# Gated-projection blocks placed inside the last batches of the state-space head, with the weight tiles in the input stage's space and W4 on another queue

## Chip, cores, metric
One core of a Trainium2 chip. The metric is device time in microseconds for one launch, median over runs; the kernel is one program with no loop at run time, every instruction is laid out in order per engine.

## What is computed
Two transformer blocks on 256 tokens of width 2048, all in float32. Only the first half of the first block is touched here: a state-space mixer (S5) followed by a gated projection.

```
sh1, sc1, gt1, sh2, sc2, gt2 = split(silu(c) @ w_mod + b_mod, 6)
h   = rms_norm(x) * (1 + sc1) + sh1                      # also for the context tokens
for both directions:  s_t = lam * s_(t-1) + B u_t        # 128 groups of 16 channels, 64 complex states
                      y  += real(C s_t)
z   = gelu(y + d * u)
a, g = split(z @ w_glu, 2)                               # w_glu is 2048 x 4096
x   = x + gt1 * rms_norm(a * sigmoid(g))
h   = rms_norm(x) * (1 + sc2) + sh2                      # goes into a 2048-8192-2048 MLP, then gt2
```

## The kernel before
**The head** (`head`, L139). The 128 groups are done in four batches of 32. A batch `b` has four generators from `s5_batch` (L375): `m` modulates the input (needs the modulation vectors from `mod_matmul`), `e` builds the input matrices X, transposes them and multiplies them with u in eight steps, `s` is the scan over chunks on DVE, `z` makes the outputs in eight steps. ORDER (L41) says in what order the program calls them; "e2+z0" alternates a step of each. The head stands in a block whose instructions a planner then reorders: it simulates the timeline and gives each engine its next ready instruction, earlier program order first.

One step of `z` (L556 to L592): DVE builds Z (three products, L403); ACT copies parts of B into bm (L566); PE multiplies bm with Z into a bank `pk` (L571, L575); ACT copies that to Kp (L578); four DMAs of 64 KB each spread Kp into the tile W4 (L582, on ACT's queue); ACT copies the states into SN (L585, L586). Two steps later (ZLAG = 2) `product` (L544) multiplies Z, SN, u and W4 into a bank `py` (L552) and ACT applies the gelu (L554). `pk`, `py` and the final transposes share the two banks of the tag "py". When a batch is through, PE transposes its result (L598) and ACT and DVE split it into a high part `zh` (L604) and a low part `zl` (L605). These are four of the sixteen k-tiles that the gated projection multiplies with; they are listed in `za`.

Beside this the head computes the vectors gt1 and sc2 (`mod_vectors`, L291): 32 steps, each with two loads of 512 KB and eight matmuls (L303), called from `z` by the digits of WORK (L36): two per step of batches 0 and 1.

**The dense part** (`Dense`, L611). Weights stream in chunks of 512 KB (`load`, L618): SP issues the load into a `raw` tile (L681), ACT casts it to the high half `wh` (L628), DVE subtracts for the low half `wl` (L629), PE does three matmuls for each pair of tiles (L657): a chunk is 24 matmuls of 128x256. `block` (L647) does one 512-wide block of outputs in eight chunks. The gated projection (L893 to L903) is three pairs of 512-wide blocks and two pairs of 256-wide ones: 64 chunks, 1536 matmuls. `glu_out` (L861) evicts a pair. `dn.fill` (L850) puts a step of `ModVectors.steps` (L330) after every second chunk: a 512 KB load `wv` on SP, and a multiply-and-sum on DVE (L338) for the vector sh2, 32 steps. The vector `cond` that it needs is loaded and put through Silu at L327 and L328, after the head.

**Memory.** In the head `raw` has four tiles that all weight loads share; after it another pool `raw2` has six. PSUM: four banks "ps" (used by `m` and `e`), two "py", two "ab" (`mod_matmul`, `mod_vectors`); after the head a new pool takes all eight.

Of the kernel before, what the change touches and what calls it, by code (L numbers as in the profile page):

```python
# [35 lines left out]
WORK = ("22222222", "22222222", "00000000", "00000000")  # L36
# [3 lines left out]
DPOOL = "BCEG"  # L40
ORDER = "m0:1 e0:4 c0 m0 e0 m1:1 s0 e1:4 m1 e1 m2 e2+z0:4 s1 m3 e2+z0 e3+z1:4 s2 e3+z1 s3 z2 z3"  # L41


class K:
    def __init__(self, ctx, tc, aps):
# [4 lines left out]
        self.psp = None  # L50
# [88 lines left out]
def head(k, raw, ctx):  # L139
# [17 lines left out]
    with ExitStack() as bx:  # L157
        b1, b2 = (bx.enter_context(tc.tile_pool(name=f"b{n}", bufs=n, reuse_waits="tile")) for n in (1, 2))
        pools = b1, b2, b3
# [21 lines left out]
        for b in range(NB):  # L181
            for i in range(2):
# [137 lines left out]
class ModVectors:  # L320


    def __init__(self, k, pool):
        self.k, nc, c = k, k.nc, k.a["c"]
        self.part = {v: k.cp.tile([P, 2, KT], F32, name=f"mvp{v}") for v in (3, 5)}
        self.cond = pool.tile([P, 2, 1024], F32, tag="hid", name="cond")
# [3 lines left out]
    def steps(self, raw, v):  # L330

        nc = self.k.nc
        for kt in range(KT):
            for h in range(2):
                t = raw.tile([P, 1024], F32, tag="raw", name=f"wv{v}_{kt}_{h}")
# [39 lines left out]
def s5_batch(k, pools, act, za, b, rs, ub, Q, R, WP, dd, bms, acc, ahead, work):  # L375

    nc, a = k.nc, k.a
    b1, b2, b3 = pools
# [5 lines left out]
    def build(tag, s, pw, pd, m, conj):  # L384
# [6 lines left out]
        else:  # L391
            out = [b3.tile([P, 4, L * 16], F32, tag=tag, name=f"{tag}{b}_{s}_{t}", bufs=XBUFS) for t in range(3)]
# [14 lines left out]
    def modulate():  # L407
        Bt = tl["B"] = b2.tile([P, 3, GB, 16], F32, tag="B", name=f"B{b}", bufs=3)
        Bx = tl["Bx"] = b2.tile([P, GB, 16], F32, tag="Bx", name=f"Bx{b}")
        nc.scalar.dma_start(Bt[:, 0:2], a["s5_b"][b])  # L410
        qd = tl["qd"] = b2.tile([P, GB, L], F32, tag="qd", name=f"qd{b}")
# [44 lines left out]
    def inputs():  # L456
        EC = tl["EC"] = b1.tile([P, NC_, 2, GB], F32, tag="EC", name=f"EC{b}")
        EL = tl["EL"] = b2.tile([P, NC_, 2, GB], F32, tag="EL", name=f"EL{b}", bufs=3)
        for s in range(GB // 4):
            X = build("X", s, Q, tl["qd"], (tl["Bx"], tl["B"][:, 2], tl["B"][:, 1]), False)  # L460
            W1 = []
            for t in range(3):
# [3 lines left out]
                w = b3.tile([P, 4, P], F32, tag="W1", name=f"W1{b}_{s}_{t}", bufs=4)  # L466
# [60 lines left out]
    def outputs():  # L527
# [28 lines left out]
        for s in range(GB // 4):  # L556
# [23 lines left out]
            for q in range(4):  # L580
                v = Kp[32 * q : 32 * q + 16, 7:15, :]
                nc.scalar.dma_start(W4[:, q, :], bass.AP(v.tensor, v.offset, [v.ap[0], [-16, L], [1, P]]))  # L582
# [10 lines left out]
        for w in wait:  # L593
            product(*w)
        pzs = [k.ps("py") for _ in range(2)]
# [15 lines left out]
class Dense:  # L611
# [20 lines left out]
    def preload(self, src, n=3, wide=512):  # L632

        self.ahead = [self.load(src, i * (1024 // wide), wide) for i in range(n)]
# [12 lines left out]
    def block(self, src, acts, pre=None, wide=512):  # L647

        k, nc = self.k, self.k.nc
        acc = [k.ps() for _ in range(wide // T)]  # L650
        nk = len(acts)
        for kt, hi, lo in self.chunks(src, nk, wide, pre):
            xh, xl = acts[kt]
            for nt in range(wide // P):
                o = acc[nt // 2][:, (nt % 2) * T : (nt % 2 + 1) * T]
                for i, (w, x) in enumerate(((hi, xh), (hi, xl), (lo, xh))):
                    nc.tensor.matmul(o, lhsT=w[:, nt * P : (nt + 1) * P], rhs=x,  # L657
                                     start=(kt == 0 and nt % 2 == 0 and i == 0),
                                     stop=(kt == nk - 1 and nt % 2 == 1 and i == 2))
        return acc  # L660

    def block_t(self, src, acts):
# [11 lines left out]
        return acc  # L674

# [87 lines left out]
def body(ctx, tc, aps):  # L763
# [5 lines left out]
    k.psum(hx, "psh", {"ps": 4, "py": 2, "ab": 2})  # L769
# [8 lines left out]

    with hx:
        k.ctx_head = hx  # L780
        raw = hx.enter_context(tc.tile_pool(name="raw", bufs=4))
        with tc.block(schedule_with_timeline_sim=True):
            za, vecs, act = head(k, raw, ctx)
# [640 lines left out]
```

## Time and profile before

| | us |
|---|---|
| median of three runs | 3377.5 |
| lowest, highest | 3375.14, 3381.65 |
| the profiled execution | 3383.99 |
| its span | 3382.1 |
| mean granted TensorE clock of the span | 0.981 |

A clock of 1.00 is 2.4 GHz, one of 0.50 is 1.2 GHz, a value between them is a mixture over the stretch. Engines: PE is the matmul, PEld the load of its stationary operand, DVE, ACT and POOL the elementwise engines, SP issues DMAs; a "q" behind the name is the engine's queue of instructions that don't compute. "[3.33 <-DMA W<-Kp]" behind a row says how long the engine was idle before it and what ended that. The program's names lose trailing digits: W is W4 and W1, wv the loads of modulation weights, wm those of `mod_matmul`.

### The profile page before, as it was taken

The numbers are of one execution on the slowest core, as the hardware profiler recorded it, in microseconds if no ns is written. First come the engines' busy times: TensorE is split into PE (matmuls) and PEld (weight loads), VectorE is DVE, ScalarE is ACT, GpSimd is POOL, SyncE is SP. The second block draws the span as 40 slices with busy tenths as digits, with TensorE's granted clock in tenths as the row PEclk, the third lists the DMA queues.
The fourth block names the chain that finished last, engine by engine and source line by source line (L and its number), as shares of the span: only waits on it lengthen the run. The fifth ranks groups of instructions, "written<-read, shape, count | busy, mean of one in ns | idle before, by whom it ended". The sixth has DMA issues, their size and how long they took to land.

```text
span 3382.1 us, 69851 instructions
## 1 busy us (share of the span) xinstructions
PE 3217.1 (95%) x30126; PEld 3080.4 (91%) x30126; DVE 2049.5 (61%) x2699; ACT 1461.2 (43%) x1785; POOL 213.0 (6%) x117
## 2 busy tenths in 40 slices
PE   7989669899999999989999999999999999999998
PEld 3567559889999999988999999999999999999998
DVE  8688736785565555689555545555556455555555
ACT  4345445444444434435544434434444443443343
POOL 0000010110000000167300000000000000000000
PEclk9999779999999999989999999999999999999999
DMA  9855267756767565445455555555535555565553
GB/s 311 286 177 177 44 196 272 242 164 230 237 229 231 187 187 187 161 152 166 158 172 187 186 188 186 188 187 187 187 120 187 176 187 187 187 187 187 187 186 139
DMA packets 355141, 642.01 MB, mean 190 GB/s; under 512 B 23184, under 2 KB 94608, under 8 KB 354448
## 3 DMA queue, kind: packets, MB, share of 16 engines
q1 hardware_dynamic: 331824, 620.19, 55.7%
q10 hardware_dynamic: 23008, 17.37, 2.3%
q8 instruction: 235, 3.85, 0.4%
q14 instruction: 74, 0.61, 0.0%
HBM read 626.96 MB, written 2.10 MB: 186 GB/s over the span
## 4 chain that ended last, share of the span: by engine, by line
PE 54%; DVE 1%; issue 0%; ACT 0%; POOL 0%; DVEq 0%; ACTq 0%; POOLq 0%
PE ps L657 52%; PE ps L672 1%; PE ps L1269 0%; POOL wl L629 0%; PE ps L746 0%; DVE xT L1243 0%; PE ps L759 0%; PE ps L1294 0%; PE ps L1053 0%; PE ps L1130 0%; DVE pq L1286 0%; PE ps L1048 0%; PE ps L66 0%; DVE fl L1307 0%; DVE wl L629 0%
## 5 line engine op out<-in xcount | busy, mean ns | idle before, releaser
L629 DVE TENSOR_TENSOR wl<-wr,wh 128x1024 fp32r<-128x1024 f32 x907 | 1115.6, 1232 | 1022.8 <-ACT wh L628 1022.1
L628 ACT CAST wh<-wr 128x1024 fp32r<-128x1024 f32 x976 | 1023.0, 1049 | 1503.6 <-PE ps L657 1372.9
L657 PE MATMUL ps<-f,wh 128*128 128x256 f32 x5632 | 997.2, 280 | 0.0
L657 PEld LDWEIGHTS ps<-f,wh 128*128 128x128 f32 x5632 | 862.3, 188 | 0.1
L657 PE MATMUL ps<-f,wl 128*128 128x256 f32 x2816 | 789.9, 281 | 0.0
L657 PEld LDWEIGHTS ps<-f,wl 128*128 128x128 f32 x2816 | 529.2, 188 | 0.0
L657 PE MATMUL ps<-m,wh 128*128 128x256 f32 x2048 | 366.4, 281 | 8.8 <-DVE m L939 5.7
L657 PE MATMUL ps<-hd,wh 128*128 128x256 f32 x2048 | 360.6, 280 | 0.0
L657 PEld LDWEIGHTS ps<-m,wh 128*128 128x128 f32 x2048 | 315.2, 189 | 10.9 <-DVE m L939 7.0
L657 PEld LDWEIGHTS ps<-hd,wh 128*128 128x128 f32 x2048 | 312.7, 188 | 0.0
L657 PE MATMUL ps<-m,wl 128*128 128x256 f32 x1024 | 287.7, 281 | 0.0
L657 PE MATMUL ps<-hd,wl 128*128 128x256 f32 x1024 | 286.7, 280 | 0.0
L657 PE MATMUL ps<-f1d,wh 128*128 128x256 f32 x1408 | 249.0, 280 | 0.0
L657 PE MATMUL ps<-f0d,wh 128*128 128x256 f32 x1408 | 247.9, 280 | 0.0
L657 PEld LDWEIGHTS ps<-f1d,wh 128*128 128x128 f32 x1408 | 215.3, 188 | 0.0
L657 PEld LDWEIGHTS ps<-f0d,wh 128*128 128x128 f32 x1408 | 215.0, 188 | 0.0
L657 PE MATMUL ps<-f1d,wl 128*128 128x256 f32 x704 | 197.3, 280 | 0.0
L657 PE MATMUL ps<-f0d,wl 128*128 128x256 f32 x704 | 197.1, 280 | 0.0
L657 PEld LDWEIGHTS ps<-m,wl 128*128 128x128 f32 x1024 | 193.2, 189 | 0.0
L657 PEld LDWEIGHTS ps<-hd,wl 128*128 128x128 f32 x1024 | 192.6, 188 | 0.0
L657 PE MATMUL ps<-z,wh 128*128 128x256 f32 x1024 | 184.4, 283 | 7.6 <-ACT wh L628 7.6
L629 POOL TENSOR_TENSOR wl<-wr,wh 128x1024 fp32r<-128x1024 f32 x69 | 167.7, 2441 | 113.6 <-ACT wh L628 106.5
(479 smaller groups left out, 4434.4 us busy)
## 6 DMA issues: line engine op xcount, KB each, us to landing
wr<-in_ffn_w_gate_dram SPq DMA_DIRECT2D x176, 512.0 KB, 3.5
wr<-in_ffn_w_up_dram SPq DMA_DIRECT2D x176, 512.0 KB, 3.5
wr<-in_ffn_w_down_dram SPq DMA_DIRECT2D x176, 512.0 KB, 3.6
wr<-in_w_mlp_in_dram SPq DMA_DIRECT2D x128, 512.0 KB, 4.2
wr<-in_w_mlp_out_dram SPq DMA_DIRECT2D x128, 512.0 KB, 4.5
wv<-in_w_mod_dram SPq DMA_DIRECT2D x64, 512.0 KB, 5.3
wr<-in_s_w_glu_dram SPq DMA_DIRECT2D x64, 512.0 KB, 5.2
wv<-in_w_modt_dram SPq DMA_DIRECT2D x64, 512.0 KB, 4.6
```

The source lines that it names most:

```text
L628: nc.scalar.copy(hi, t)
L629: self.low(n).tensor_tensor(lo, t, hi.bitcast(F32), op=ALU.subtract)
L657: nc.tensor.matmul(o, lhsT=w[:, nt * P : (nt + 1) * P], rhs=x, start=(kt == 0 and nt % 2 == 0 and i == 0), stop=(kt == nk - 1 and nt % 2 = ...
L672: nc.tensor.matmul(acc[tt], lhsT=x[:, tk], rhs=w, start=(kt == 0 and i == 0), stop=(kt == nk - 1 and i == 2))
```

## The change
The gated projection's first three blocks are started inside the head. After `e3+z1` the item "w" closes a pool `xw` (into which X, W1, Bx and qd have moved) and opens the pool `wp` of weight halves in its space. From then on a side step "g" is called once per round: it loads one chunk and does its 24 matmuls for k-tiles that are already in `za`, for the first or second block (banks "ps"), or, when both vectors are done, for the third (banks "ab"). In the last batch two side steps "v" per round do `ModVectors` for sh2, whose `cond` is now loaded at the start of the head. By the order of calls 20 chunks and 22 steps of sh2 fall into the head. W4 of batches 2 and 3 is issued by SP. The scan s3 alternates with z2. WORK spreads the steps of `mod_vectors` over batches 0, 1 and 2 (8, 16, 8). After the head, blocks preload two chunks of the next block before the eviction of a pair; the sums of squares of x go from POOL to DVE (DPOOL) and are moved.

```diff
-WORK = ("22222222", "22222222", "00000000", "00000000")
+WORK = ("11111111", "22222222", "11111111", "00000000")
-DPOOL = "BCEG"
-ORDER = "m0:1 e0:4 c0 m0 e0 m1:1 s0 e1:4 m1 e1 m2 e2+z0:4 s1 m3 e2+z0 e3+z1:4 s2 e3+z1 s3 z2 z3"
+DPOOL = "BEG"
+SIDE = {"g": 1, "v": 2}
+ORDER = "m0:1 e0:4 c0 m0 e0 m1:1 s0 e1:4 m1 e1 m2 e2+z0:4 s1 m3 e2+z0 e3+z1:4 s2 e3+z1 w s3+z2+g z3+g+v"
...
+        if self.ring:
+            tag = self.ring[0]
+            self.ring = self.ring[1:] + self.ring[:1]
...
+        xx = ctx.enter_context(ExitStack())
+        xw = xx.enter_context(tc.tile_pool(name="xw", bufs=1, side="right", reuse_waits="tile"))
+        pools = b1, b2, b3, xw
...
+        vec = k.vec = ModVectors(k)
...
+        side = {}
         for item in ORDER.split():
+            if item == "w":
+                xx.close()
+                side["g"] = start(za, lambda: len(vecs) == 2)
+                side["v"] = k.vec_work = vec.steps(3)
+                continue
             names, n = (item.split(":") + ["99"])[:2]
-            gens = [bt[int(t[1])][t[0]] for t in names.split("+")]
+            names = names.split("+")
+            gens = [bt[int(t[1])][t[0]] for t in names if t not in side]
             for _ in range(int(n)):
                 gens = [g for g in gens if not next(g, 1)]
+                for t in names:
+                    for _ in range(SIDE[t] if t in side else 0):
+                        next(side[t], None)
+                if not gens:
+                    break
...
-                nc.scalar.dma_start(W4[:, q, :], ...)
+                (nc.sync if b >= 2 else nc.scalar).dma_start(W4[:, q, :], ...)
...
         for w in wait:
             product(*w)
+        yield
...
-    def preload(self, src, n=3, wide=512):
+    def preload(self, src, n=3, wide=512, first=0):
...
+class Run:
+    def __init__(self, dn, src, nk, wide=512, tag="ps"):
+        self.dn, self.src, self.nk, self.wide, self.kc = dn, src, nk, wide, 0
+        self.acc = [dn.k.ps(tag) for _ in range(wide // T)]
+    def step(self, acts, pre=None):
+        dn, nc = self.dn, self.dn.k.nc
+        st = 1024 // self.wide
+        hi, lo = dn.ahead.pop(0) if dn.ahead else dn.load(self.src, self.kc, self.wide)
+        if pre:
+            pre(self.kc)
+        if dn.fill:
+            dn.fill()
...
+        self.kc += st
...
-    k.psum(hx, "psh", {"ps": 4, "py": 2, "ab": 2})
+    k.psum(ctx, "psh", {"ps": 4, "py": 2, "ab": 2})
...
+    def start(za, free):
+        dn = Dense(k, raw, ctx.enter_context(tc.tile_pool(name="wp", bufs=3, side="right", reuse_waits="tile")))
+        dense.append(dn)
+        while True:
+            if len(runs) < 2:
+                runs.append(Run(dn, glu_srcs[len(runs)], KT))
+            run = next((r for r in runs if r.kc < len(za)), None)
+            if not run and len(runs) == 2 and free():
+                run = Run(dn, glu_srcs[2], KT, tag="ab")
+                runs.append(run)
+            if run:
+                run.step(za)
+            yield
...
-    k.psum(ctx, "psd", {"ps": 8})
+    k.ring = ["py", "py", "ps", "ps", "ps", "ps", "ab", "ab"]
...
-    dn.preload(plain_src(nc, a["s5_w_glu"], D))
...
+    def ahead():
+        if order:
+            i = order.pop(0)
+            dn.preload(glu_srcs[i], 2, 512 if i < 6 else 256)
+        else:
+            dn.preload(w_in[0], 2)
...
+    def glu(i):
+        if i < len(runs):
+            r = runs[i]
+        else:
+            r = Run(dn, glu_srcs[i], KT, 512 if i < 6 else 256)
+            runs.append(r)
+        while not r.done():
+            r.step(za)
+            if r.done() and i + 1 >= begun:
+                ahead()
+        return r.acc
+    begun = len(runs)
+    for i in range(begun):
+        glu(i)
+    dn.fill = every(2, work)
+    stream_squares()
     for i in range(3):
-        pg = dn.block(plain_src(nc, wglu, D + 512 * i), za)
-        if i == 0:
+        glu_out(i, 4, glu(2 * i), lambda: glu(2 * i + 1), 4 * i)
+        if i == 1:
             stream_sums()
-        glu_out(i, 4, pg, lambda: dn.block(plain_src(nc, wglu, 512 * i), za), 4 * i)
...
-    work = vec.steps(raw, 5)
-    w_in = [plain_src(nc, a["w_mlp_in"], 512 * j) for j in range(16)]
-    dn.preload(w_in[0])
+    work = vec.steps(5)
...
-    nc = bacc.Bacc("TRN2", target_bir_lowering=False, num_devices=1)
+    nc = bacc.Bacc("TRN2", target_bir_lowering=False, num_devices=1, dynamic_dma_scratch_size=1024)
```

## Rows read from the trace of the kernel before

**Rows 1.** The page: the span, and busy time of PE.
```profile
span 3382.1 us, 69851 instructions
PE 3217.1 (95%) x30126; PEld 3080.4 (91%) x30126; DVE 2049.5 (61%) x2699; ACT 1461.2 (43%) x1785; POOL 213.0 (6%) x117
```

**Rows 2.** Busy time by stretch (us, engines with instructions, clock, DMA share, GB/s).
```profile
200.00:339.00 139.00, 128.57 (x2575) 103.22 (x2568) 124.22 (x253) 74.85 (x157) 0.00 (x0) 0.98 0.60 187
339.00:459.00 120.00, 70.95 (x2002) 60.28 (x1991) 63.97 (x124) 47.82 (x103) 0.00 (x0) 0.79 0.36 74
464.00:665.00 201.00, 187.39 (x1539) 185.12 (x1540) 141.23 (x155) 103.89 (x146) 23.80 (x11) 0.97 0.77 262
665.00:712.00 47.00, 32.44 (x229) 29.57 (x228) 42.51 (x94) 19.16 (x34) 12.05 (x5) 0.93 0.30 91
```

**Rows 3.** Timeline of ACT, one step of the last batch (start, us).
```profile
431.00 0.28 ACT L554 ACTIVATE u<-py 128x128 f32<-128x128 f32 x1 [3.33 <-DMA W<-Kp]
...
433.34 0.36 ACT L578 COPY Kp<-py 128x240 f32<-128x240 f32 x1
433.73 3.27 ACTq L582 DMA_DIRECT2D W<-Kp  x4
437.04 0.28 ACT L554 ACTIVATE u<-py 128x128 f32<-128x128 f32 x1 [3.34 <-DMA W<-Kp]
```

**Rows 4.** Timeline of PE, another step of that batch.
```profile
421.69 1.63 PE L571 MATMUL py<-Z,bm 128*32 128x128 f32 x72 [1.14 <-ACT Kp L578]
...
425.30 1.08 PE L552 MATMUL py<-Z,SN 128*32 128x128 f32 x32 [1.94 <-ACT u L554]
...
426.19 0.40 PE L552 MATMUL py<-W,u 128*32 128x128 f32 x8
```

**Rows 5.** PE's dense matmuls in 40 us, and groups of lines from 465 to 660.
```profile
560.00:600.00 40.00, 38.62 (x335) 38.41 (x334) 1.00 0.80 273
...
L629 DVE TENSOR_TENSOR wl<-wr,wh 128x1024 fp32r<-128x1024 f32 x64 | 82.2, 1313 | 1.8 <-ACT wh L628 1.8
L338 DVE SCALAR_TENSOR_TENSOR wv<-wv,cond 128x1024 f32<-128x1024 f32 x31 | 41.4, 1336 | 54.9 <-DMA wv<-in_w_modt_dram 54.9
```

**Rows 6.** Timeline of PE: one step of `mod_vectors`.
```profile
125.17 1.07 PE L303 MATMUL ab<-wv,st 128*32 128x512 f32 x8
```

**Rows 7.** DMA queues (packets, MB, share of 16 engines): 404 to 440, then 580 to 600.
```profile
q10 hardware_dynamic: 3456, 1.57, 31.0%
...
q1 hardware_dynamic: 2620, 6.06, 86.0%
```

**Rows 8.** W4's transfers from issue to landing: whole kernel, then 440 to 460.
```profile
DMA to landing us min/median/max: 2.4/3.0/8.1
...
DMA to landing us min/median/max: 3.0/7.2/7.8
```

**Rows 9.** Timeline of ACT and PE between the head and the first block.
```profile
458.63 1.28 ACT L328 ACT_TABLE_LOAD   x1
461.20 1.91 ACT L328 ACTIVATE cond<-cond 128x2048 f32<-128x2048 f32 x1 [1.29 <-DMA cond<-in_c_dram]
...
464.10 0.80 PE L657 MATMUL ps<-z,wh 128*128 128x256 f32 x2 [7.57 <-ACT wh L628]
```

**Rows 10.** Waits (us in total, times, longest): 460 to 640, then 60 to 200.
```profile
PE ps L657 <- DVE wl L629: 11.7, 6, 5.8
...
PEld ab L368 <- DMA wm<-in_w_mod_dram: 14.1, 14, 2.8
...
PEld ab L303 <- DMA wv<-in_w_mod_dram: 8.5, 8, 1.3
```

**Rows 11.** Waits of SP's queue, 0 to 470.
```profile
SPq L300 <- PE ab L303: 116.0, 24, 17.5
```

**Rows 12.** Timeline of ACT and PE at the end of the gated projection.
```profile
665.20 1.05 ACT L628 CAST wh<-wr 128x1024 fp32r<-128x1024 f32 x1 [1.78 <-PE ps L657]
...
673.46 0.67 PE L759 MATMUL ps<-spm,ones 128*128 128x256 f32 x2 [3.59 <-DVE rr L925]
```

More of the change, by code (lines that the diff above doesn't have):

```diff
@@ L49, in __init__ @@
         self.cp = ctx.enter_context(tc.tile_pool(name="cp", bufs=1))
-        self.psp = None
+        self.psp, self.ring = None, None
         self.ident = self.cp.tile([P, P], F32, name="ident")
@@ L136, in cmul, with head @@
     eng.tensor_tensor(out[:, :, 1, :], out[:, :, 1, :], tmp[:, :, 1, :], op=ALU.add)
-def head(k, raw, ctx):
+def head(k, raw, ctx, start):
     nc, tc, a = k.nc, k.tc, k.a
@@ L320, with __init__, steps @@
 class ModVectors:
-    def __init__(self, k, pool):
+    def __init__(self, k):
         self.k, nc, c = k, k.nc, k.a["c"]
         self.part = {v: k.cp.tile([P, 2, KT], F32, name=f"mvp{v}") for v in (3, 5)}
-        self.cond = pool.tile([P, 2, 1024], F32, tag="hid", name="cond")
+        self.cond = k.cp.tile([P, 2, 1024], F32, name="condb")
         nc.scalar.dma_start(self.cond.rearrange("p h n -> p (h n)"), bass.AP(c.tensor, c.offset, [[0, P], [1, 2048]]))
         nc.scalar.activation(self.cond, self.cond, AF.Silu)
-    def steps(self, raw, v):
+    def steps(self, v):
         nc = self.k.nc
@@ L334, in steps @@
             for h in range(2):
-                t = raw.tile([P, 1024], F32, tag="raw", name=f"wv{v}_{kt}_{h}")
+                t = self.k.raw.tile([P, 1024], F32, tag="raw", name=f"wv{v}_{kt}_{h}")
                 r = v // 2 * D - D + kt * P
@@ L391, in build @@
         else:
-            out = [b3.tile([P, 4, L * 16], F32, tag=tag, name=f"{tag}{b}_{s}_{t}", bufs=XBUFS) for t in range(3)]
+            out = [xw.tile([P, 4, L * 16], F32, tag=tag, name=f"{tag}{b}_{s}_{t}", bufs=XBUFS) for t in range(3)]
         gl = slice(4 * s, 4 * s + 4)
@@ L630, in load @@
         return hi, lo
-    def preload(self, src, n=3, wide=512):
-        self.ahead = [self.load(src, i * (1024 // wide), wide) for i in range(n)]
+    def preload(self, src, n=3, wide=512, first=0):
+        self.ahead = [self.load(src, first + i * (1024 // wide), wide) for i in range(n)]
     def chunks(self, src, nk, wide, pre):
@@ L645, in chunks, with block @@
                 yield kc + a, hi[:, a], lo[:, a]
[L647 to L660, printed above, removed]
+    def block(self, src, acts, pre=None, wide=512, then=None):
+        r = Run(self, src, len(acts), wide)
+        while not r.done():
+            r.step(acts, pre)
+            if r.kc == len(acts) and then:
+                then()
+        return r.acc
     def block_t(self, src, acts):
@@ L674, in block_t, with done @@
         return acc
+class Run:
+    def __init__(self, dn, src, nk, wide=512, tag="ps"):
+        self.dn, self.src, self.nk, self.wide, self.kc = dn, src, nk, wide, 0
+        self.acc = [dn.k.ps(tag) for _ in range(wide // T)]
+    def done(self):
+        return self.kc == self.nk
+    def step(self, acts, pre=None):
[6 more added lines that the diff above has]
+            dn.fill()
+        for a in range(st):
+            kt = self.kc + a
+            xh, xl = acts[kt]
+            for nt in range(self.wide // P):
+                o = self.acc[nt // 2][:, (nt % 2) * T : (nt % 2 + 1) * T]
+                for i, (w, x) in enumerate(((hi, xh), (hi, xl), (lo, xh))):
+                    nc.tensor.matmul(o, lhsT=w[:, a, nt * P : (nt + 1) * P], rhs=x,
+                                     start=(kt == 0 and nt % 2 == 0 and i == 0),
+                                     stop=(kt == self.nk - 1 and nt % 2 == 1 and i == 2))
+        self.kc += st
 def plain_src(nc, w, n0, k0=0):
@@ L834, in stream_sums @@
         fold(nc, s_x)
+    def stream_sums():
         ps = k.ps()
@@ L847, in every @@
         return f
-    work = vec.steps(raw, 3)
-    dn.fill = every(2, work)
+    work = k.vec_work
+    w_in = [plain_src(nc, a["w_mlp_in"], 512 * j) for j in range(16)]
+    order = list(range(len(runs), len(glu_srcs)))
+    def ahead():
[4 more added lines that the diff above has]
+            dn.preload(w_in[0], 2)
     y = mp.tile([P, KT, T], F32, tag="y", name="y1")
@@ L891, in glu_out @@
         return [o[:, 0] for o in (tx, ty, tq)]
+    def glu(i):
[4 more added lines that the diff above has]
+            runs.append(r)
+        while not r.done():
+            r.step(za)
+            if r.done() and i + 1 >= begun:
+                ahead()
+        return r.acc
+    begun = len(runs)
[3 more added lines that the diff above has]
+    stream_squares()
     for i in range(3):
[L894 to L895 removed]
+        glu_out(i, 4, glu(2 * i), lambda: glu(2 * i + 1), 4 * i)
+        if i == 1:
             stream_sums()
[L897 removed]
     for i in (12, 14):
```

33 lines of the change are left out of this document (17 added, 16 removed).

## The prediction
> **What bounds the kernel now.** I read the page first: PE is busy 95% of the span [rows 1], so the average says that only fewer or faster matmuls help. An average hides stages, so next I read busy time by stretch [rows 2]. From 464 to 665 us, the gated projection, PE is busy 187 of 201 us at nearly full clock: there time is what PE has to do. But from 339 us, when the last input stage is through, to 459 us, when the last batch's result is split, PE is busy 71 of 120 us, at a mean clock of 0.79, DVE 64 us, ACT 48 us, and the DMA engines 36%. No engine is full there, so something serial sets the pace. The timeline of ACT shows it for the last batch [rows 3]: gelu to gelu takes 6.04 us, and 3.27 us of that is ACT issuing the four W4 transfers, during which it computes nothing and everything behind it on its queue waits. The same step needs PE for only 1.65 us (bm with Z) and 1.29 us (the product) at full clock [rows 4], about 3.0 us. So half of these 120 us is free PE time, and the stage that follows is bound by PE.
>
> **The change, part by part.** The sum is made against the profiled execution, 3384.0 us (span 3382.1), which is 6.5 us above the median of 3377.5.
>
> (1) Moved matmuls. 20 of the projection's 64 chunks go into the head. The stage takes 201 / 64 = 3.14 us a chunk with its stalls [rows 2], so it loses 20 x 3.14 = 62.8 us.
>
> (2) The price in the head, from 339 us. I add up each resource. PE: 16 steps x 3.0 = 47 us and 2 us of transposes at full clock, 8 steps of `mod_vectors` moved here x 1.07 [rows 6] = 9 us, 20 chunks of 24 matmuls at 40 / 335 = 0.119 us [rows 5] = 57 us; together 115 us. DVE: the 64 us it had, 20 low halves x about 1.25 and 22 products for sh2 x about 1.3 (the means of 1.31 and 1.34 [rows 5] hold slow ones beside POOL, which is idle in the head) = 25 + 29; together 118 us. DMA: 20 + 22 + 16 loads of 0.524 MB = 30.4 MB; 6.06 MB took 86% of 20 us [rows 7], so 353 GB/s at full use and 86 us; the W4 packets took 0.31 x 36 x 16 / 3456 = 0.052 us each, and 64 transfers of 128 packets over 16 engines are 27 us; together 113 us. ACT: 48 us and 20 casts of 1.05 us [rows 12], 69 us. Three resources stand within 5 us of each other at about the 120 us that the stretch has now, so it can't stay at 120. In the busiest stretch before it, 200 to 339 us, the planner got 124 of 139 us out of DVE, 89% [rows 2]; 118 / 0.89 = 132 us, and at the end the last W4 transfer and the final split run alone, some 6 us more than that share already holds. I take 138 us: **+18 us**. Bounds: 120 us (0), if the pieces interlock, and 155 us (+35), which is DVE at 76%. What covers the moved matmuls is PE waiting; if that cover were gone they would cost their 57 us again.
>
> (3) W4 on SP. ACT loses up to 16 x 3.3 = 52 us of issue [rows 3]; with it ACT would be at 69 + 52 = 121 us, a fourth full resource, so this part is what makes (2) possible. Its gain is in (2). SP must now issue these 64 transfers between 58 loads, and SP stands still whenever a load has no free `raw` tile: longest wait 17.5 us [rows 11]. Behind a waiting load stand W4, the next loads, and on PE the product of that step with all dense matmuls behind it. The product comes two steps later, at 138 / 16 = 8.6 us a step, so 17 us are covered. W4 landed in 3.0 us when alone and in 7.2 us when weight loads ran beside it [rows 8], both from ACT's queue. I take 8 us, hidden except at the ends of the two batches, which (2) holds; bounds 0 and the rival below. The Trainium skill (DMA: Bandwidth & Descriptors, Queues, rings and completion order) speaks against this: SP and ACT have a ring each on the same 16 engines, one ring is consumed in order, and the engines alternate between rings, so on SP's ring W4 stands behind every load issued before it. By that rule, an estimate from that page's order and the measured rate, four outstanding loads of 1.5 us and the 2.4 us of a lone transfer make 8.4 us to landing, and the sum would be half a microsecond worse; at its worst the rule is the rival of the caught W4 below.
>
> (4) `cond` leaves the transition. Between the split of the last batch and PE's first dense matmul ACT loaded a table, waited for `cond` and did Silu on it, and the first cast stood behind that: PE was idle for 7.57 us and began at 464.1 [rows 9]. This goes: -4 us (bounds 0 and -5). At the start of the head the same 1 MB is loaded, and Silu takes 1.9 us of ACT. DMA-limited, 1 MB costs 1.05 / 0.353 = 3 us: +3 (bounds 0 and +5).
>
> (5) `mod_vectors`, 8 steps out of batch 0. Batch 0's steps run while PE waits for modulation weights: 14.1 us for wm, 8.5 us for wv, 60 to 200 us [rows 10]. 8.4 MB less there is 24 us of DMA time, but most of it is hidden by PE and DVE: I take -4 (bounds 0 and -12).
>
> (6) Block boundaries. PE waited 11.7 us at six places for low halves [rows 10]; 44 of 64 chunks stay, 8 us of it, and two chunks ready before each eviction should save half: -4 (bounds 0 and -8). At the end the first MLP chunks are cast before the last eviction, ahead of the chain of sums that PE waits for (3.59 us of idle at its largest [rows 12]): two casts and two low halves at most, +2 (bounds 0 and +4). xT is squared on ACT earlier; its transfer has the remaining chunks to land, six of them at 2.9 us: 0. DVE takes three additions from POOL, in a stage where it is busy 141 of 201 us and loses 29 us of work for sh2: 0. The pool and PSUM renaming issue nothing.
>
> Sum: -62.8 + 18 - 4 + 3 - 4 - 4 + 2 = **-52 us**, that is 3332 in such an execution and 3377.5 - 52 = 3325.5, say 3326, as a median.
>
> **Rivals.** *The head gives it back.* DVE, PE and DMA are all at their limit at once, and in-order engines block each other: a low half that DVE does late holds PE, and PE the batch's products. Then the stretch takes 160 to 180 us instead of 138; at 175 us the sum is -52 + 37 = -15, 3362. For it: three sums within 5 us of each other. Against: 89% on two engines just before. Chance 0.14.
>
> *Slower: W4 caught behind loads that wait.* Place: SP's queue from 339 us. A load of weights waits there for a `raw` tile that is freed only by DVE or PE, and these wait, through the product, for the W4 behind it. Price: break-even is 52 us above my 138, 190 us, or 11.9 us a step; with two steps of cover that takes 24 us from Kp to landing. The longest single wait of SP (17.5 us) and the longest landing (8.1 us) together make 25.6 us [rows 8, 11], so it is possible; if every step met it, 16 x 12.8 = 205 us, +15, 3392. Against: the long waits were a planned pace, not a jam. Chance 0.08.
>
> *It isn't done.* The planner puts the dense chunks behind the batches because the batches come first in its order. Then only W4 helps: eight steps fall from 6.0 to about 4 us, -16, with (4) to (6) -23: 3354. Against: PE is idle for half of the time, and it takes what is ready. Chance 0.03. Something between all these within 0.2%: 0.04.
>
> **How the numbers follow.** The forecast with its bounds has 0.71: best -62.8 + 0 - 5 + 0 - 12 - 8 + 0 = -88, worst of it -62.8 + 35 + 0 + 5 + 0 + 0 + 4 = -19. The range for 8 in 10 is 3294 to 3363: it reaches from the near-best case to the rival of the stretched head and leaves out the jam. Faster by over 0.2% (6.8 us, about what a measurement here can tell from nothing): 0.71 + 0.14 + 0.03 = 0.88; within it 0.04; slower 0.08.
>
> **What would show it.** In the profile of the changed kernel: dense matmuls (some 480) before the last batch's split; a clock near 1.0 in the stretch that had 0.79; W4 on SP and no ACT gap of 3.3 us behind Kp; the time from the last input step to the last split about 138 us; from there to the end of the projection about 44 x 2.9 = 128 us and few waits for wl; 4 us or less between split and dense matmul. I am wrong in (2) if that stretch is over 155 us, in (3) if products wait for W4 in the middle of a batch, in (5) if the stretch before moved by more than 12 us.

## The result, and the profile after

The changed kernel takes 3416.74 us (median of four runs) against 3379.57 us for the kernel before on the same chip: a ratio of 1.0108, 95% interval 1.0088 to 1.0128. It is slower, where 3326 us were predicted. One of the four, 3536.96 us, ran at a granted clock of 0.849 and is left out of the ratio; the other three lie between 3415.18 and 3417.29 us. The two profiled executions show where, by the points that both programs pass:

| point (us) | before | after | difference |
|---|---|---|---|
| last matmul of the input stage | 335.4 | 341.4 | +6.0 |
| end of the head's last split | 459.8 | 507.2 | +47.4 |
| last matmul of the gated projection | 665.0 | 652.8 | -12.2 |
| first matmul of the MLP | 677.1 | 667.2 | -9.9 |
| last product of the second feed-forward layer | 3368.7 | 3402.2 | +33.5 |

So in these executions the touched part gains 9.9 us, and the untouched rest of the program loses 43.4. First the touched part. Busy time by stretch of the changed kernel, columns as in [rows 2], and in the last row 100 us of the first feed-forward layer:

```profile
200.00:341.00 141.00, 126.25 (x2607) 107.43 (x2604) 124.48 (x255) 78.24 (x164) 0.00 (x0) 0.96 0.40 117
341.00:432.00 91.00, 77.36 (x1437) 59.85 (x1434) 72.97 (x129) 44.56 (x79) 0.00 (x0) 0.95 0.71 214
432.00:456.00 24.00, 24.00 (x246) 23.22 (x246) 11.97 (x15) 6.99 (x9) 0.00 (x0) 0.90 0.50 178
456.00:507.00 51.00, 36.69 (x941) 31.29 (x939) 33.72 (x53) 18.79 (x40) 0.00 (x0) 0.85 0.92 282
507.00:653.00 146.00, 138.92 (x1108) 138.10 (x1109) 91.10 (x97) 83.66 (x127) 12.57 (x8) 0.96 0.67 221
...
2000.00:2100.00 100.00, 100.00 (x836) 100.00 (x835) 51.41 (x47) 39.23 (x38) 0.00 (x0) 1.00 0.58 182
```

Read the rows from 341 us against the second of [rows 2]. The mean clock is 0.95 to 432 us, close to what was hoped. Then PE does some seven chunks in a row (164 dense matmuls) with hardly a step of the last batch (24.00 of 24.00 us, 246 instructions), and from 456 to 507 us it does that batch's steps with two chunks of dense work left beside them, at 0.92 of the DMA engines. The order of work ran out of cover before its last and longest chain was through. Between 200 and 341 us, on the other hand, the DMA share fell from 0.60 [rows 2] to 0.40: 11 steps of `mod_vectors` ran there instead of 21, and 10 of the 32 steps were left for the time behind 341 us. WORK had planned eight there. Their loads stand in SP's queue until the step before them has run (waits up to 507 us; us in total, times, longest):

```profile
SPq L319 <- PE ab L322: 98.4, 24, 40.6
SPq L319 <- DMA W<-Kp: 50.4, 5, 29.5
```

The longest wait is 40.6 us, where [rows 11] had 17.5; both this one and the 29.5 lie between 200 and 341 us. Behind the head, the timelines of PE and ACT (start, us):

```profile
506.06 0.79 PE L715 MATMUL ps<-z,wh 128*128 128x256 f32 x2 [2.13 <-ACT z L624]
...
517.72 0.74 PE L715 MATMUL ps<-z,wh 128*128 128x256 f32 x4 [2.67 <-ACT wh L648]
```

```profile
515.67 1.06 ACT L892 ACTIVATE s_x<-xT 128x1024 f32<-128x1024 f32 x1 [9.67 <-DMA xT<-in_xt_dram]
516.64 2.92 ACT L648 CAST wh<-wr 128x1024 fp32r<-128x1024 f32 x3
```

The first dense matmul comes right at the split: PE stood 2.13 us before it, not 7.57 [rows 9]. But ACT then stands 9.67 us for xT, three casts behind it, and PE runs dry.

Now the rest. The same 100 us of the same stage in the kernel before:

```profile
2000.00:2100.00 100.00, 100.00 (x852) 100.00 (x852) 50.55 (x46) 40.54 (x39) 0.00 (x0) 1.00 0.60 186
```

PE is never idle in either, and the granted clock is 1.00 in both, the 2.4 GHz level. Yet PE gets through 852 matmuls before and 836 after. This is a cost that no wait shows: every matmul is a little further from the next, 100 / 836 = 119.6 ns instead of 117.4. For some tiles the load of the stationary operand takes longer too (its duration in ns, min/median/max; the first row is before, the others after):

```profile
L657 PEld LDWEIGHTS ps<-f,wh x5632: 186/188/332, 1739.3 to 3294.5; 128*128 128x128 f32 x195
```

```profile
L715 PEld LDWEIGHTS ps<-f,wh x2816: 187/192/193, 1747.9 to 3282.0; 128*128 128x128 f32 x188
...
L715 PEld LDWEIGHTS ps<-hd,wh x1024: 187/187/193, 794.4 to 1393.2; 128*128 128x128 f32 x171
```

With the hidden tiles (hd) the load takes what it took before, and yet the matmuls are 120.0 ns apart there too (table further down), so a longer load is not what sets the distance. Behind the projection stand 21,504 dense matmuls; 21,504 x 2.25 ns = 48 us, which is the loss and a little more.

### The profile page after: what moved, and what is told of

Read it like the earlier page. It is cut to its first block, busy times and chain, and to the rows that moved or that the text cites. A ratio compares the mean times of both kernels' runs of the same rounds, so it can differ in the third digit from the quotient of the medians.

```text
span 3415.3 us, 69893 instructions
## 1 busy us (share of the span) xinstructions
PE 3272.7 (96%) x30126; PEld 3131.4 (92%) x30126; DVE 2048.9 (60%) x2701; ACT 1459.0 (43%) x1786; POOL 204.1 (6%) x115
## 4 chain that ended last, share of the span: by engine, by line
PE 79%; DVE 2%; issue 1%; POOL 1%; ACT 1%; DVEq 0%; ACTq 0%; POOLq 0%
PE ps L715 37%; PE py L715 21%; PE ab L715 20%; POOL wl L649 1%; PE ps L686 0%; DVE m L1026 0%; DVE c L866 0%; PE ps L1356 0%; DVE xT L1094 0%; DVE xs L1023 0%; PE ab L790 0%; ACT wh L648 0%; PE ps L790 0%; DVE pq L1373 0%; PE ab L803 0%
## 5 line engine op out<-in xcount | busy, mean ns | idle before, releaser
L715 PE MATMUL ps<-f,wh 128*128 128x256 f32 x2816 | 507.4, 283 | 0.0
L715 PEld LDWEIGHTS ps<-f,wh 128*128 128x128 f32 x2816 | 439.3, 192 | 0.0
L715 PE MATMUL ps<-f,wl 128*128 128x256 f32 x1408 | 398.4, 283 | 0.0
L715 PE MATMUL py<-f,wh 128*128 128x256 f32 x1536 | 277.2, 283 | 0.0
L715 PEld LDWEIGHTS ps<-f,wl 128*128 128x128 f32 x1408 | 270.3, 192 | 0.0
L715 PEld LDWEIGHTS py<-f,wh 128*128 128x128 f32 x1536 | 239.6, 192 | 0.1
L715 PE MATMUL ab<-f,wh 128*128 128x256 f32 x1280 | 230.8, 283 | 0.0
L715 PE MATMUL py<-f,wl 128*128 128x256 f32 x768 | 217.7, 283 | 0.0
L715 PEld LDWEIGHTS ab<-f,wh 128*128 128x128 f32 x1280 | 199.7, 192 | 0.0
L715 PE MATMUL ps<-m,wh 128*128 128x256 f32 x1024 | 184.5, 283 | 0.0
```

Source lines behind the costliest of these rows:

```text
L715: nc.tensor.matmul(o, lhsT=w[:, a, nt * P : (nt + 1) * P], rhs=x, start=(kt == 0 and nt % 2 == 0 and i == 0), stop=(kt == self.nk - 1 and ...
```

## Experiments on the later stages

Three things that the change does reach into the later stages: the weight tiles lie on the right side of SBUF, under the activations; the PSUM banks come in a ring of three names; the DMA scratch is smaller, so that everything on the left lies 15 KB lower. Each was done alone. A ratio always stands for the kernel before timed beside the run; its median lay between 3374 and 3383 us, so that from one group of runs to another ratios are compared, not microseconds.

**Weight tiles on the right**, in the kernel before:

```diff
-    wp = ctx.enter_context(tc.tile_pool(name="wp", bufs=3, reuse_waits="tile"))
+    wp = ctx.enter_context(tc.tile_pool(name="wp", bufs=3, side="right", reuse_waits="tile"))
```

> The kernel before, with only the weight-half tiles put on the right side of SBUF, directly under the tiles of the activations, as in the changed kernel. Theory P (place): the later stages of the changed kernel run 835 matmuls per 100 us where the kernel before runs 852, because weight halves and activations now lie side by side; then this kernel runs about 836 per 100 us after 700 us, and as it keeps the order of the kernel before in the head, it takes about 45 to 50 us more, 3425 us. Rival B (the PSUM banks, handed out in a ring over the head's pool) and rival S (the left side moved down by 15 KB with the small DMA scratch): no change, 852 per 100 us and 3380 us within 5.

Measured: 3429.78 us, ratio 1.0154 (1.0133 to 1.0175). The window:

```profile
2000.00:2100.00 100.00, 100.00 (x836) 100.00 (x835) 49.78 (x46) 38.55 (x37) 0.00 (x0) 1.00 0.62 182
```

**Weight tiles back on the left** after the head, in the changed kernel: `wp` is opened in the head's own stack, and behind `raw2` a pool `wp2` is opened on the left.

```diff
+    wp2 = ctx.enter_context(tc.tile_pool(name="wp2", bufs=3, reuse_waits="tile"))
...
+    dn.wp = wp2
```

> The changed kernel, whose weight halves move back to the left side (behind the raw tiles) once the head is over; the projection in the head stays on the right side. Theory P: 852 matmuls per 100 us again after 700 us, which gives back some 40 us: about 3373 us, a little under the kernel before, by the 10 us that the projection ends earlier. Rivals B and S: the rate stays at 836 and the time at 3417 us within 5.

Measured: 3359.16 us, ratio 0.9947 (0.9928 to 0.9965); 3373 had been expected. Two of its windows are used further down:

```profile
0.00:100.00 100.00, 72.20 (x644) 35.54 (x645) 77.63 (x219) 41.60 (x60) 1.20 (x7) 0.90 0.85 285
...
200.00:300.00 100.00, 85.35 (x1795) 74.09 (x1796) 88.82 (x175) 51.65 (x109) 0.00 (x0) 0.97 0.31 87
...
2000.00:2100.00 100.00, 100.00 (x851) 100.00 (x851) 53.57 (x48) 40.64 (x40) 0.00 (x0) 1.00 0.64 187
```

**The ring and the scratch**, each alone in the kernel before:

```diff
-    k.psum(hx, "psh", {"ps": 4, "py": 2, "ab": 2})
+    k.psum(ctx, "psh", {"ps": 4, "py": 2, "ab": 2})
-    k.psum(ctx, "psd", {"ps": 8})
+    k.ring = ["py", "py", "ps", "ps", "ps", "ps", "ab", "ab"]
```

> The kernel before, with only the PSUM pool changed: the head's eight banks under three names are kept to the end and handed out in a ring, as in the changed kernel. Rival B: 836 matmuls per 100 us after 700 us and about 3425 us. Theory P and rival S: 852 and 3380 us within 5.

```diff
+    nc = bacc.Bacc("TRN2", target_bir_lowering=False, num_devices=1, dynamic_dma_scratch_size=1024)
```

> The kernel before, with only the DMA scratch cut from 16 KB to 1 KB, which moves everything on the left side of SBUF down by 15 KB. Rival S: 836 matmuls per 100 us after 700 us and about 3425 us. Theory P and rival B: 852 and 3380 us within 5.

Measured: the ring 3366.20 us, 0.9964 (0.9945 to 0.9983), at 851 in the same window; the scratch 3373.32 us, 0.9995 (0.9981 to 1.0009), at 852. Neither slows the later stages; the ring even gains some 12 us, which I had not expected and did not take apart. Of the three, the move of the weight tiles makes the loss, and its undoing takes it away.

**The place, or the address?** The left and the right differ in more than place. By the program's allocation (the traces hold no addresses) the tiles began at 45728 bytes of each partition, which is 32 more than a multiple of 128, and now begin at 172000, which is 96 more; the activations begin at 196576, also 96. A tile of 64 bytes tells the two apart:

```diff
+    pad = ctx.enter_context(tc.tile_pool(name="pad", bufs=1, side="right"))
+    nc.gpsimd.memset(pad.tile([P, 16], F32, name="pad"), 0.0)
     wp = ctx.enter_context(tc.tile_pool(name="wp", bufs=3, side="right", reuse_waits="tile"))
```

> As b_wp_right, with a tile of 64 bytes between the activations and the weight halves, so that these begin at 171936, at the same remainder of 128 (32) as in the kernel before. Theory P1 (where they lie counts): still 836 matmuls per 100 us after 700 us. Rival P2 (their remainder of 128 counts): 852 per 100 us.

One run: 3387.18 us, where the kernel before had 3374.74 to 3386.15, and the window

```profile
2000.00:2100.00 100.00, 100.00 (x852) 100.00 (x851) 50.50 (x46) 40.58 (x39) 0.00 (x0) 1.00 0.64 186
```

So theory P fell in the form in which I had stated it: the place on the right costs nothing, 64 bytes of address do. The same 64 bytes in the changed kernel:

> The changed kernel with nothing but a tile of 64 bytes ahead of the weight halves, which then begin at remainder 32 of 128 bytes, as in the kernel before, and stay on the right side. Theory P2 (the remainder of the weight tiles' address is the whole cost of the later stages): 852 matmuls per 100 us after 700 us, and 3359 us within 5, as a_wp_left, which moved them to another place with the same remainder. Rival P3 (the two earlier runs agree by chance, the changed kernel has another cause): 836 and 3417 us.

Measured: 3359.52 us, 0.9953 (0.9941 to 0.9966). The window:

```profile
2000.00:2100.00 100.00, 100.00 (x852) 100.00 (x851) 54.59 (x50) 40.51 (x39) 0.00 (x0) 1.00 0.64 187
```

That is the whole of the loss, given back by one empty tile.

**Other remainders.** The kernel before with 96 bytes ahead of the weight tiles (remainder 0):

> The kernel before, with a tile of 96 bytes ahead of the weight halves, which then begin at a multiple of 128 bytes (45824) instead of remainder 32. Theory P2 (the remainder sets the rate: 852 per 100 us at 32, 836 at 96): the rate changes again; if the weight load is cheapest on a whole boundary, to about 890 (the 444 per 50 us that a stretch of a_wp_left showed), and the time falls by up to 100 us, to 3280; if remainders under 64 are alike, it stays at 852 and 3380 us. Theory P1 is already out; it too would expect 852.

Measured: 3389.93 us, 1.0032 (1.0018 to 1.0045), 848 in the window: a third rate, and no gain from a whole boundary. Then the remainders the other way round, weights at 96 and activations at 32:

```diff
+    pad0 = ctx.enter_context(tc.tile_pool(name="pad0", bufs=1, side="right"))
+    pad0.tile([P, 16], F32, name="pad0")
     act = ctx.enter_context(tc.tile_pool(name="act", bufs=1, side="right", reuse_waits="tile"))
...
+    pad = ctx.enter_context(tc.tile_pool(name="pad", bufs=1))
+    nc.gpsimd.memset(pad.tile([P, 16], F32, name="pad"), 0.0)
     wp = ctx.enter_context(tc.tile_pool(name="wp", bufs=3, reuse_waits="tile"))
```

> The kernel before with 64 bytes ahead of the weight halves on the left (remainder 96 instead of 32) and 64 bytes ahead of the activations on the right (remainder 32 instead of 96). Theory P2a (the weight tiles' own remainder counts): 836 matmuls per 100 us in the stages that multiply with the activations, about 3425 us. Theory P2b (it counts against that of the activations: slow where both are alike): 852 and 3380 us.

One run: 3341.95 us, faster than either expected. The windows of the first and of the second layer:

```profile
2000.00:2100.00 100.00, 100.00 (x884) 100.00 (x884) 55.26 (x52) 43.67 (x42) 0.00 (x0) 1.00 0.66 194
2650.00:2750.00 100.00, 100.00 (x851) 100.00 (x851) 52.67 (x47) 41.19 (x40) 0.00 (x0) 1.00 0.64 185
```

Remainder 96 of the weights is thus not slow by itself; the pair counts. Five rounds of the same kernel:

> The same kernel as b_act32, timed in five rounds. In its one look the mean distance of two matmuls in the MLP and the first feed-forward layer was 113.3 ns where the kernel before has 117.8 at the opposite remainders. Theory A (the pair of remainders, weights 96 and activations 32, brings the short distance): the time stays near 3342 us, a ratio of about 0.99. Rival C (two distances are possible at this pair as at the other, and the one look drew the short one by chance): the runs scatter between 3340 and 3385 us with a median above 3360.

Measured: 3347.79 us, 0.9918 (0.9892 to 0.9944), single runs from 3334 to 3363. Theory A holds for the median, and rival C for the scatter, which is wider than that of any kernel above. Tiles: m is the MLP's input, hd its hidden tiles, f the input and f0d and f1d the hidden tiles of the two feed-forward layers. The starts of successive dense matmuls in all these traces, averaged over 10 us at a time (gaps over 200 ns left out), take only a few values:

| weights, moving operand (bytes over a multiple of 128) | difference | where | ns |
|---|---|---|---|
| 96, 96 | 0 | the changed kernel, b_wp_right: m, f | 120.0 |
| 96, 64 | 32 | the same: hd, f0d, f1d | 120.0 |
| 0, 96 | 32 | b_wp0: m, f | 118.3 |
| 32, 96 | 64 | before, a_wp_left, b_wp_right64, a_pad64: m, f | 117.8; 113.3 in some stretches of a_wp_left and a_pad64 |
| 96, 32 | 64 | b_act32, e_act32: m, f | 113.3 in m and the first layer's f, 117.8 in the second layer's |
| 32, 64 | 96 | before and the others of row 4: hd, f0d, f1d | 117.3; 118.7 at times |
| 96, 0 and 0, 32 | 96 | b_act32, e_act32; b_wp0: hd, f0d, f1d | 117.3; 118.7 at times |

Ordered by how far the weights' remainder lies ahead of the moving operand's (modulo 128), differences 0 and 32 are slow on the whole, and at 64 there are two values. It is an order, not a law: at 32 one pair gives 120.0 and the other 118.3, which is less than the 118.7 that occurs at 96; and it was read from these eight pairs, not tried on a new one. Nor do these runs tell remainders of 128 bytes from those of 256. A value holds for a stage or a large part of it. It changes at pauses of the stream of matmuls, at a change of the moving tile, and in a_wp_left, a_order and d_best_w4 within m without a gap over 200 ns; why, no run here shows. Which of the two values a run gets matters when runs are compared: b_psum_ring, b_scratch, a_pad64 and c_early have 140 to 150 us of f at 113.3 ns, the trace of the kernel before has none, and that is worth 5 to 6 us.

## Experiments on the head

These start from a_wp_left, so that the later stages are out of the way. There the last split stood at 506.1 us (the start of its last step, here and below; the table at the top has its end, 1.1 us later).

**The modulation loads**, back at two steps per step of the first two batches:

```diff
-WORK = ("11111111", "22222222", "11111111", "00000000")
+WORK = ("22222222", "22222222", "00000000", "00000000")
```

> a_wp_left with the modulation loads back at two steps per step of the first two batches, as in the kernel before. Theory T1: the pause of the loads between 240 and 300 us (a DMA share of 0.31 there) pushed a third of them into the stretch of the last two batches, where they take transfers and PE time; undone, 200 to 300 us shows a DMA share of about 0.6 again, the third block is free earlier, and the last split of the head moves from 506 to about 497 us: some 8 us less than a_wp_left, 3351 us. Rival T2: the stretch is bound by its order, the third batch's steps and the scan first and the last batch's steps behind them with little dense work left; then the split stays within 4 us of 506.

Measured: 3350.64 us, 0.9908 (0.9889 to 0.9926), last split at 490.4 us. The gap in the transfers is gone (compare the row of a_wp_left above, DMA share 0.31):

```profile
200.00:300.00 100.00, 94.84 (x1889) 73.72 (x1888) 91.58 (x183) 52.48 (x111) 0.00 (x0) 1.00 0.62 198
```

T1 holds; the split moved by 16 us where 9 were expected.

**The scan at double pace** (its generator named twice in a round):

```diff
-... w s3+z2+g z3+g+v"
+... w s3+s3+z2+g z3+g+v"
```

> a_wp_left with the last scan driven at two steps per round, so that it ends with the third batch's eight steps and the last batch's begin some four rounds earlier, with eight chunks of the dense work left for them instead of six or fewer. Theory T2 (the order binds the stretch): the last split moves from 506 to about 490 us, the granted clock of the last 50 us of the head rises from 0.85 to above 0.95, and the time is some 12 us under a_wp_left, 3347 us. Rival T3 (transfers bind it: modulation loads, weight gathers and dense chunks at a DMA share of 0.9): the split stays within 5 us of 506.

Measured: 3359.89 us, 0.9932 (0.9914 to 0.9949), split at 506.6: nothing at the split, as T3 has it.

**The conditioning row later**, its load after the second batch's input steps, its Silu before the third's:

> a_wp_left with the load of the conditioning row (1 MB broadcast) and its Silu taken from the kernel's first microseconds to just before the third batch's modulation. Theory T4: that load holds up the start (648 matmuls recorded in the first 100 us against 801 with the start of the kernel before); without it about 800, the last matmul of the input stage comes at 331 us instead of 339, and the time is some 7 us under a_wp_left, 3352 us. Rival: the start's lag comes from the input tiles on the right side and their fewer buffers; then the count stays near 650.

Measured: 3357.02 us, 0.9930 (0.9912 to 0.9948); last input matmul at 332.6 instead of 339.0, split at 500.3.

```profile
0.00:100.00 100.00, 74.71 (x702) 37.41 (x703) 79.06 (x226) 43.34 (x64) 1.20 (x7) 0.97 0.90 304
```

702 matmuls, between 644 and the expected 800: the load is a third to a half of the early lag, and neither expectation holds. The 6.4 us at the end of the input stage are not all its work, because that point scatters from trace to trace: 326.5 to 336.6 us with the start of the kernel before (eight traces), 336.6 to 341.4 where the row is loaded first, as in the changed kernel (six), 332.6 to 339.3 where it is loaded later (six). By the medians the start lost 7.5 us and the later load gives 3 back. The ratio moved by 0.0017 (some 6 us) against a_wp_left, and the two intervals overlap.

**W4 on ACT again**, in a_work:

```diff
-                (nc.sync if b >= 2 else nc.scalar).dma_start(W4[:, q, :], ...)
+                nc.scalar.dma_start(W4[:, q, :], ...)
```

> a_work with the gathers of W4 of the last two batches put back on ACT's queue. By term 1 of the prediction (an issue costs ACT 3.27 us per step, in the way of the chain) the last split moves from 490 to about 525 us and the time rises by some 30 us to 3380. Rival Q: ACT has room beside (busy 40% of the stretch) and SP's queue delays the gathers by as much as they held up ACT; then the split stays within 6 us of 490 and the time within 8 us of 3351.

(What this text calls term 1 stands in part (3) of the prediction.) Measured: 3349.62 us, 0.9912 (0.9892 to 0.9932) against 3350.64; split at 497.4, 7.0 us later, of which 2.9 were there at the end of the input stage. Rival Q holds for the time and misses its 6 us at the split by one: the queue is worth some 4 us at most, and nothing in the time.

**Spreading the sh2 steps**, with both edits that helped:

```diff
-SIDE = {"g": 1, "v": 2}
+SIDE = {"g": 1, "v": 1}
-... w s3+z2+g z3+g+v"
+... w s3+z2+g+v z3+g+v"
```

> a_work and a_cond together, and the modulation steps of the head (v) spread at one per round over both of the last batches' rounds, instead of two per round beside the last batch alone. Theory T3 (transfers bind the last batch's steps, DMA share 0.85 to 0.91 at 430 to 490 us): the last split moves from 490 to about 475 us, of which the start gives 6, and the time is some 12 us under a_work, 3338. Theory T2 (the order binds): only the start's 6 us are gained, 484 us and 3345.

Measured: 3350.54 us, 0.9915 (0.9900 to 0.9930), split at 493.5. The DMA share of the last steps fell, first a_work, then this run:

```profile
460.00:490.00 30.00, 17.71 (x479) 15.51 (x478) 19.66 (x32) 10.87 (x22) 0.00 (x0) 0.82 0.85 246
...
460.00:490.00 30.00, 20.75 (x682) 18.31 (x680) 15.32 (x24) 14.39 (x31) 0.00 (x0) 0.83 0.65 150
```

But there is no gain over a_work, so T3 fails here; T2's 484 and 3345 were missed too. And with the scan at double pace on top ("s3+s3+z2+g+v"):

> c_spread with the last scan driven at two steps per round, so that the last batch's steps begin four rounds earlier. Theory T2, now that the modulation loads are out of the way: the last split moves to about 465 us, and the time to about 3330. Theory T3: as c_spread, within 4 us.

Measured: 3337.59 us, 0.9884 (0.9862 to 0.9905), split at 484.1, where T2 expected 3330 and 465. Of the 9.4 us at the split, 4.4 were there at the last input matmul, which this edit does not touch; the stretch itself shrank by 5.0. So the order that did nothing alone gains 5 us in the stretch once the modulation loads are out of its way: that a_order's batch still waited for those loads is the likely reason, but only argued. The time gains 13 us, of which some 5 may come from stretches at 113.3 ns (c_spread's trace has none in f). What is left shows in PE's waits from 335 to 500 us:

```profile
PE py L575 <- DMA W<-Kp: 15.3, 9, 5.3
```

**The squares of x later**, behind four chunks of the fourth block, and **W4 of the last batch on ACT**; both on a_pad64 with all edits of c_early:

```diff
     dn.fill = every(2, work)
+    runs.append(Run(dn, glu_srcs[3], KT))
+    for _ in range(4):
+        runs[3].step(za)
     stream_squares()
```

> a_pad64 with the edits that helped, together: the modulation loads as in the kernel before (a_work), the conditioning row later (a_cond), one modulation step per round over both batches and the last scan at two steps per round (c_early); and four chunks of the fourth block put ahead of the squares of x, so that ACT does not wait for x with the casts behind it. c_early took 3338 us with 5.2 us of PE waiting for a cast at 515 us: if that wait is what the early squares cost, it goes, and the time is about 3332 us. If the wait only moves to the next use of x, it stays at 3338.

> d_best with W4 of the last batch back on ACT's queue (that of the third batch stays on SP's). In c_early PE waited 15.3 us for W4 in the stretch. Theory Q1 (the gathers wait in SP's queue behind loads that wait for a tile): PE's waits for W4 fall below 6 us, the last split comes some 5 to 10 us earlier, about 3325 us. Rival Q2 (ACT's issue of 3.3 us per step costs as much): within 4 us of d_best.

Measured: 3343.58 us, 0.9898 (0.9883 to 0.9913), and 3343.61 us, 0.9912 (0.9893 to 0.9930). No gain from either. Against c_early, whose weights lie on the left, d_best also has the base a_pad64. Without the early squares PE's wait of 5.2 us for a cast became one of 3.3 us for a cast and one of 2.7 for a low half; and W4 on ACT left PE's waits for it at 15.7 us (16.5 in d_best), so Q1 fell.

**Both together**: c_early with the remainders of b_act32.

> c_early (weights at 32 and activations at 96 after the head, 3338 us) with the activations at remainder 32, the weights after the head at 96 and the MLP's hidden tiles at 0, as in b_act32. Theory A: the stages up to 2590 us run at 113.3 ns again and the time falls by some 30 us, to about 3307 us. Rival C: 117.8 ns in most of them and 3338 us within 6.

Measured: 3310.42 us, ratio 0.9794 (0.9771 to 0.9818), the best here: 64 us under the kernel before and, by the ratios, 106 under the changed one. Its windows, of the first and of the second layer:

```profile
2000.00:2100.00 100.00, 100.00 (x885) 100.00 (x884) 55.21 (x50) 42.07 (x42) 0.00 (x0) 1.00 0.67 195
2650.00:2750.00 100.00, 100.00 (x851) 100.00 (x850) 53.91 (x49) 40.48 (x39) 0.00 (x0) 1.00 0.63 190
```

In this execution the MLP ran at 117.8 ns, where e_act32 had 113.3, and the single runs lie between 3296 and 3322 us: rival C again, within theory A.

## Why the prediction was wrong

**The step that failed** is the last sentence of part (6): "The pool and PSUM renaming issue nothing." That is true of instructions, and I made it a cost of 0. But the pool of the weight tiles also got another address, and 21,504 matmuls behind the projection became 2.25 ns dearer each. b_wp_right makes the loss without the rest of the change (+52 us), a_pad64 takes it away with 64 bytes (the ratio falls from 1.0108 to 0.9953, some 52 us). No rival of mine had a place for it; each looked only at the head. Without it the change is faster than before, by 0.5%: the sign of the forecast was right for the part that I had looked at, its size, 16 us instead of 52, was not; that is parts (2) and (5).

By parts, in the profiled executions:

(1) Moved matmuls. Only 18 chunks ran before the split (434 dense matmuls, where 20 chunks are 480). The projection lost 201 - 146 = 55 us; 18 x 3.14 = 56.5. The price per chunk was right, the count was not: the first three batches deliver k-tiles for 3 x 6 chunks, and the last two that were counted need those that the last batch delivers only at its split. Nor are the 4 us of part (6) for block boundaries in these 55.

(2) The head's stretch, from the last input matmul to the end of the split, took 165.8 us. The kernel before takes 124.4 between these points, where I had counted 120, so my 138 stands for 142 here and the bound of 155 for 159. The growth is 41.4 us instead of 18: the second largest miss, +23 us. I had summed each resource over the whole stretch and taken the fullest. (The step of bm with Z takes 1.63 us in [rows 4], not 1.65; nothing hangs on it.) The rows show that the work was not there when the resource was free: seven chunks ran in a row before the last batch's steps. With the modulation loads early the stretch is 491.5 - 337.1 = 154 us, with the scan at double pace too (c_early) 485.2 - 334.9 = 150, inside the bound. The rival "the head gives it back" named the size, 160 to 180 us, but three full resources as the reason. Of that reason the transfers are answered in part: c_spread took the DMA share of the last steps from 0.85 to 0.65 and moved nothing. DVE and PE were not relieved alone in any run, so that the order is the cause of the 23 us is argued, with c_early's 5 us as the part that was shown.

(3) W4 on SP. The 64 gathers on SP landed in a median of 4.7 us (3.0 in [rows 8]), at most 6.9; 8 had been allowed. The jam did not happen. But the sentence that this move "is what makes (2) possible" is wrong: c_w4act shows the stretch without it, 4 us longer at most. Once PE had other work, ACT's issue of 3.27 us a step [rows 3] cost those 4 us and not the 52 of its sum. The rule of the Trainium skill that part (3) weighed (DMA: Bandwidth & Descriptors, Queues, rings and completion order) would have W4 wait behind each earlier load on its ring; PE's waits for W4 of 12.7 us in a_work as in c_w4act agree with neither queue being better.

(4) The transition gained its 4 us. The start lost 6 us in these two executions and 7.5 by the medians of all traces, not 3; the later load of a_cond gives back about the 3 that were priced. What the rest is, no run shows; the input tiles on the right with fewer buffers, the rival of a_cond, stay untested.

(5) The modulation steps out of batch 0: -4 had been taken, and the stretch before moved by +6 in all; putting them back (a_work) moved its end by -1.9, inside the scatter of that point, so the -4 was not there. The price of the same eight steps behind 341 us stood in (2) as 9 us of PE and 16 loads, and cost nothing there, since DVE was the fullest resource. They cost 14 us: a_work's split is 15.7 us earlier, 1.9 of it before the stretch. The two together had the wrong sign.

(6) xT squares: 0 had been taken, since six chunks were to cover xT. The wait for the casts behind it is 2.67 us of PE at 517.72. d_best shows that moving the squares alone does not get it back.

The sum, by the table and so for these two executions alone: expected -52, measured +33. Of the 85 us between, 43 are the later stages, 23 the stretch of the head, 7 the start, 11 the projection with its two ends.

## What to carry to other kernels

Before pricing a change of pools at nothing, compare the rate of a stage that it does not touch, in matmuls per 100 us at full clock, in both traces. Here a difference with PE at 100% in both was an address, and a tile of 64 bytes tests that in one run. A sum over a stretch does not see in what order its work comes: here the cover was used up before the end of the chain. An edit that does nothing alone (the double pace of the scan) can be worth a second try when the wait ahead of it is gone. And before a few microseconds at one point are put down to an edit, compare that point in several traces of the same kernel: the input stage ended at 326.5 us in b_act32 and at 336.6 in e_act32, which are one program.

## What the runs showed of the hardware that was not expected

The distance of two 128x256 matmuls, each with its own weight load, depends on the start addresses of both SBUF operands: 120.0, 118.7, 118.3, 117.8, 117.3 or 113.3 ns by their remainders of 128 bytes, at a granted clock of 1.00 in all windows shown. The duration of the weight load does not follow it: 192 ns at remainders 96 and 96 against 188 before, but 187 at 96 and 64, where the distance is 120.0 as well. The Trainium skill (SBUF — State Buffer, A bandwidth-pool intuition that's wrong (but worth ruling out)) gives the weight load a second, independent read port; read alone, that lets one expect that the place of one operand does not matter for the other. Here it does: the pair of remainders changes the rate by up to 6% (113.3 against 120.0 ns). By what mechanism, no run shows. The same page (Operand start alignment) asks only for a multiple of the element's size, and all addresses here keep that rule; it says nothing of rates.

At weights 96 and activations 32 both 113.3 and 117.8 ns occur, for stages at a time, in the same program; single runs of such a kernel scatter by 25 to 28 us (e_best, e_act32), of the kernel before by 9 to 20. What draws the one or the other was not tried.
